# The scores of the first two neighbourhood jobs beside the last projection panels

## The chip, the cores and the metric

The kernel runs on one core of one Trainium2 chip. The metric is the device time of one execution in microseconds; three runs of the kernel before the change took 1579.09, 1581.71 and 1585.59 us, and their median, 1581.71 us, is the time before. The result must agree with a reference in JAX that works in 32-bit floats.

## The reference

Two layers of a diffusion backbone run over 512 latent tokens, on a grid 64 columns wide, and 256 context tokens, with a model width of 1024. Layer 0 projects the modulated tokens once and then attends in two groups of heads: eight latent-attention heads and eight heads of two-dimensional neighbourhood attention. A SwiGLU follows. Layer 1 has sliding-window attention and another SwiGLU. What the change touches is the neighbourhood attention of layer 0. Each latent query reads 16 columns around it, in every one of the grid's eight rows, with a bias by relative place, and all context keys, in one softmax; context queries read context keys alone. Cut to its core:

```python
p_lat = a_lat @ w_in
p_ctx = a_ctx @ w_in
...
s_lat = jnp.einsum('bnqhd,bknmhd->bhnqkm', qr, k_blk).astype(jnp.float32) * scale
s_lat = s_lat + col_bias[:, dr_idx].transpose(0, 2, 3, 1, 4)[None]
s_lat = jnp.where(col_ok[:, :, None, :], s_lat, NEG_INF).reshape(b, h, n_cb, NA_CB, kr * NA_KB)
s_ctx = jnp.einsum('bnqhd,bchd->bhnqc', qr, kc).astype(jnp.float32) * scale
p = jax.nn.softmax(jnp.concatenate([s_ctx, s_lat], axis=-1), axis=-1).astype(v.dtype)
p_lat = p[..., n_ctx:].reshape(b, h, n_cb, NA_CB, kr, NA_KB)
return (jnp.einsum('bhnqc,bchd->bnqhd', p[..., :n_ctx], vc)
        + jnp.einsum('bhnqkm,bknmhd->bnqhd', p_lat, v_blk))
```

## The kernel before

Tokens lie along the free axis, 512 latent and 256 context columns, and features on the 128 partitions. A 32-bit product is made of three matmuls, with both operands split into a rounded part and a rest (L335, L337, L338). The modulated tokens are eight such pairs, sixteen tiles of the pool `b`, which has 24 buffers; they stay until the last projection has read them.

`projections()` is a generator over twelve panels of weights (one of them narrow). A panel is worked on the latent columns (24 matmuls of 512 columns) and on the context columns (24 of 256), and the generator gives up control after every second of eight steps, so a panel has eight steps and all panels have 96. The first four panels make queries and keys of head pairs 0 and 1, the next four feed the latent heads, and the last four are the raw queries and keys of pairs 2 and 3, left in the pool `p` of eight buffers until `split_pair` splits them. Between the steps `bg()` makes the modulation vectors: VectorE multiplies and sums one half of the weights by one vector (L255, L259), GpSimd multiplies in place by the other (L272), ScalarE sums that (L273), and VectorE ends it (L275, L276).

Attention is a row of jobs (`na_jobs`, three for each of four head pairs). Job 0 of a pair does the context queries of both heads, job 1 the latent query blocks 0 and 1, job 2 the blocks 2 and 3. A job is a generator with two halves. Its front makes, for each query block, the scores on TensorE (L745, L746) into one of three banks `pss`, takes them out on VectorE with the bias added and the row minimum found (`take`, L555, into a tile of `p` or `wr`), and makes exponentials on ScalarE with their sum (`exps`, L551). The bias of a head is two tiles `nb`, loaded by DMA into a pool of two buffers; a pair needs four. The context queries of one head share a bank, one half each. After its front a job yields False; its back turns the exponentials on TensorE (L499, into banks `pst` and `psd`, two each), copies them out on VectorE or ScalarE (L490, L491), and multiplies with the values (L545).

`attend()` runs jobs with a lag of one: the front of a job is written beside the back of the one before, by a pattern of f, b and s, where s is a step of side work (the splits of later pairs, the latent norms with the root L988, its reciprocal L989 and the gain L965). Before the change the first front starts when all projections are written.

The order written in the program is a list of priorities. A scheduler goes through it with its own estimate of times and fixes each engine's order and each buffer's tenants; on the chip each engine works its list in order and waits at semaphores.

Of the kernel before, what the change touches and what calls it, by code (L numbers as in the profile page):

```python
# [2 lines left out]

# [1 line left out]

# [63 lines left out]
PATTERN = ("fbsfbsfbbsfs",) * 3  # L69
BG = ((0, 0, 0, 0, 0), (2, 3), (0, 0), (0, 0))  # L70
FIRST = 2000
STEPS = ((2, 3, 4, 4), 5, 3)
HALVES = (slice(0, 256), slice(256, 512))
SWAP8 = [(i // 16) * 16 + (i % 16 + 8) % 16 for i in range(32)]
# [24 lines left out]
def hybrid_kernel(ctx: ExitStack, tc, I, out):  # L99
# [6 lines left out]
    def T(tag, shape, dt=F32):  # L106
        count[0] += 1
        if tag not in SIZES:
            return sb.tile(shape, dt, tag=tag, name=f"{tag}_{count[0]}", bufs=BUFS.get(tag, 1))
        n = int(np.prod(shape[1:]))  # L110
        t = sb.tile([P, SIZES[tag] // (2 if dt == mybir.dt.bfloat16 else 4)], dt, tag=tag, name=f"{tag}_{count[0]}",
                    bufs=BUFS[tag])[: shape[0], :n]
        if len(shape) == 3:
            t = t.rearrange("p (a b) -> p a b", a=shape[1])
        return t

    def B(dt=F32, tag="b"):
        return T(tag, [P, NT], dt)

    def PS(tag):  # L120
        count[0] += 1
        return ps.tile([P, 512], F32, tag=tag, name=f"ps{tag}_{count[0]}", bufs=PBUFS[tag])
# [185 lines left out]
    def bg(n=1):  # L308

        for _ in range(n):  # L310
            next(mods, None)
# [213 lines left out]
    def weighted(o, lanes):  # L525
# [13 lines left out]
        for n in range(max(len(m) for m in moving)):  # L539
            for i, (v, _, all_qs) in [*enumerate(lanes)][::-1]:  # L540
                if n < len(moving[i]):
                    kt, qs, t = moving[i][-1 - n]
                    c = slice((qs[0] - all_qs[0]) * P, (qs[-1] + 1 - all_qs[0]) * P)
                    with shifted(-FIRST):
                        ins = PE.matmul(o[64 * i : 64 * i + 64, c], v(kt), t, start=n == 0, stop=n == len(moving[i]) - 1)  # L545
# [97 lines left out]
    @contextmanager  # L643
    def shifted(by):
        tc.cur_priority += by
        yield
        tc.cur_priority -= by
# [3 lines left out]
    def step(n=1):  # L651

        for _ in range(n):
            while side_work:
                try:
                    with shifted(lower[0]):
                        next(side_work[0])
                    break
                except StopIteration:
                    side_work.popleft()  # L660
# [8 lines left out]
    def attend(jobs, lag=LAG):  # L669

        todo = deque()
        outs[1] = PS("o") if PBUFS["o"] == 1 else None
        for j in jobs:
            n, units = rate[0]
            bg(int(len_jobs[0] * units) - int((len_jobs[0] - 1) * units))
            len_jobs[0] += 1
            pattern = PATTERN[phase[0]]
            sides, back, front = pattern.count("s"), todo.popleft() if len(todo) >= lag else None, True
            i = 0
            for x in pattern:  # L680
                if x == "s":
                    step((i + 1) * n // sides - i * n // sides)
                    i += 1
                elif x == "f":
                    front = front and next(j)
                elif back:
                    back = None if next(back, back) is back else back
            while front:
                front = next(j)
            if back:  # L690
                for _ in back:
                    pass
            todo.append(j)
        for j in todo:
            for _ in j:
                pass
# [45 lines left out]
    def stacked_scores(t1, ks):  # L742
        def scores(o, q, keys):
            x = t1[:, q * P : (q + 1) * P]
            PE.matmul(o, x, ks[0][:, keys], start=True, stop=False)  # L745
            PE.matmul(o, x, ks[1][:, keys], start=False, stop=True)  # L746

        return scores
# [24 lines left out]
    def keys_of(v, side, mixed=None):  # L773

        def get(kt):
            t, i = (v, kt) if kt < 6 else (mixed, kt - 6)
            return t[:, i * P + 64 * side : i * P + 64 * side + 64]

        return get
# [15 lines left out]
    def first_norm(acc, c):  # L795
        n, d = (c.stop - c.start) // P, PM()
        col = T("sm", [P, 6, 2]).rearrange("p a b -> p (a b)")[:, :n]
        ins = [PE.matmul(d[:, i : i + 1], acc[:, i * P : (i + 1) * P], ones[:, :1], start=True, stop=True) for i in range(n)]
        run(ins[0], ins[-1])
        root = S.activation(col, d[:, :n], AF.Sqrt, bias=eps, scale=1.0 / D)  # L800
        V.reciprocal(col, col)
        return root, col
# [74 lines left out]
    _, diag = first_norm(acc, LATS)  # L877
# [8 lines left out]
    for c in range(4):  # L886
# [16 lines left out]
        if c == 3:  # L903
            _, diag = first_norm(acc, CTXS)
# [31 lines left out]
    def beside(gen):  # L936
        side_work.append(gen)
        return gen
# [81 lines left out]
    def split_pair(p):  # L1020

        tag = ("b", "st")[p - 2]
        q, k = raws[2 * p - 4 : 2 * p - 2]
        how = S.copy, G.tensor_copy, V.tensor_copy
        sets.append((new_q(tag), new_k(tag)))
        put_q(sets[p][0], None, how[RQ[p - 2]], (G, V)[RL[p - 2]].tensor_tensor)(q, slice(0, NT))
        yield
        put_k(sets[p][1], KC[1], how[RK[p - 2]])(k, slice(0, NT))
        yield
# [96 lines left out]
    def mix():  # L1126

        t = B()
        for i in range(2):
            VX.append(t[:, 2 * P * i : 2 * P * i + 2 * P])  # L1130
            v = VN[len(VX) - 1]
            for r, c in ((slice(0, 64), slice(2 * P, 4 * P)), (slice(64, 128), slice(0, 2 * P))):
                G.tensor_copy(VX[-1][r], v[r, c])

    def na_jobs():
        for p in range(4):
            if p == 3:
                lower[0] = L3
            for x in ORDER[p]:
                beside(split_pair(int(x)) if x in "23" else {"n": latent_norms, "m": mla_prepare}[x]())  # L1140
            rate[0] = STEPS[0][p], BG[0][p]
            if p % 2 == 0:
                mix()
            po = B()
            sums, mins = T("sm", [P, 6, 2]), T("sm", [P, 6, 2])
            hs = []
            for s in range(2):
                t1, ks = sets[p]
                hs.append(Head(s, stacked_scores(t1[s], ks[s]), keys_of(VN[p], s, VX[p]), None, nb_tiles(2 * p + s), -LOWEST, sums, mins))
            yield from pair_jobs(hs, po, True, finish(po, sums, 6))  # L1150
            while len(sets) < min(p + 2, 4):
                step()
            ON.append(po)

    i = 0
    for _ in projections():
        i += 1
        bg(int(i * DBG) - int(i * DBG - DBG))
    dense[0] = False
    attend(na_jobs())  # L1160
    drain()

    def in_rows(src, dst=None):
# [13 lines left out]
    def mla_jobs():  # L1177
        phase[0], lower[0] = 1, LOWER
        rate[0] = STEPS[1], BG[0][4]
        ready.append(latent_operands(1))  # L1180
# [44 lines left out]
    ahead, soon = {}, []  # L1225
# [378 lines left out]
    lower[0] = LOWER  # L1604
    rate[0] = STEPS[2], 0
    attend(swa_jobs())
# [186 lines left out]
```

## Time and profile before

| what | value |
|---|---|
| median of three runs | 1581.71 us (1579.09 to 1585.59) |
| the profiled execution | 1582.8 us, its span 1581.0 us |
| granted TensorE clock, mean | 0.992 |
| 0 to 46 us, start and first norm: TensorE busy | 31.37 us, clock 0.96 |
| 46 to 176 us, values' end and projections | 128.84 of 130 us, clock 1.00 |
| 176 to 268 us, neighbourhood attention | 85.45 of 92 us, clock 0.94 |
| 268 to 370 us, latent heads | 100.82 of 102 us, clock 1.00 |

The rest, from 370 us on, is the output projection, the first SwiGLU, layer 1 and the second SwiGLU. A span runs from the first to the last instruction of the profiled execution; the device time of the same execution is 1.8 us longer. The clock is the share of full speed that TensorE was granted. A busy TensorE at half the clock counts as busy, so both columns have to be read. Lines are those of the kernel before; in the changed kernel they are two higher at first (L557 is L555, L747 is L745).

### The profile page before, as it was taken

Reading aid. Unit: us, or ns where it says so; the run is one execution under the profiler, and the core shown is the slowest. Engines: PE = TensorE matmul, PEld = TensorE weight load, DVE = VectorE, ACT = ScalarE, POOL = GpSimd, SP = SyncE. Lnnn points to the kernel's source line nnn. Section 1 sums busy time; section 2 is a strip of 40 time slices with the busy share of each in tenths; the row PEclk is TensorE's granted clock in tenths of the full one; section 3 lists DMA queues with packets and bytes.
Section 4 is the critical chain, followed back from the end, with each engine's and each line's share of the span. In section 5 each row is a group of like instructions: output and inputs, shape, how many; then the busy total and the mean of one; then the engine's idle time right before and its main releaser. Section 6 shows DMA issues by size and latency. Waiting matters only on the chain.

```text
span 1581.0 us, 26527 instructions
## 1 busy us (share of the span) xinstructions
PE 1532.9 (97%) x10024; PEld 1376.0 (87%) x10024; DVE 1174.2 (74%) x2345; ACT 795.6 (50%) x1607; POOL 275.9 (17%) x302
## 2 busy tenths in 40 slices
PE   6999999999999999999999999999999999999998
PEld 4787778887998999999989998877789899899998
DVE  3885777685678597786858676889976778678685
ACT  4563677775565243342424334548856545454453
POOL 0144624320011101002021121480012000000001
PEclk9999999999999999999999999999999999999999
DMA  9745242004444545537465585110225123323222
GB/s 313 253 130 175 77 129 73 11 7 160 155 165 144 175 156 181 198 127 273 154 252 176 171 328 191 42 52 2 62 77 170 50 98 128 94 94 127 84 98 87
DMA packets 76464, 214.91 MB, mean 136 GB/s; under 512 B 9872, under 2 KB 16400, under 8 KB 76336
## 3 DMA queue, kind: packets, MB, share of 16 engines
q1 hardware_dynamic: 59216, 144.42, 27.8%
q0 software_dynamic: 15968, 67.24, 12.2%
q8 instruction: 78, 1.28, 0.3%
q10 hardware_dynamic: 1152, 1.57, 0.3%
q14 instruction: 50, 0.41, 0.1%
HBM read 186.97 MB, written 23.07 MB: 133 GB/s over the span
## 4 chain that ended last, share of the span: by engine, by line
PE 38%; DVE 5%; issue 3%; DMA 3%; POOL 1%; ACT 1%; DVEq 0%; POOLq 0%; ACTq 0%
PE pss L1378 3%; PE pss L1376 2%; PE pss L1377 2%; PE pso L545 2%; PE pst L1378 2%; PE pst L1377 2%; PE pst L1376 2%; PE psd L335 2%; DMA rope<-in_mod_w_dram 2%; PE pss L335 2%; PE pss L337 2%; PE pss L338 2%; PE psd L337 2%; PE psd L338 2%; PE pst L337 1%
## 5 line engine op out<-in xcount | busy, mean ns | idle before, releaser
L324 ACT CAST wh<-wr 128x1024 fp32r<-128x1024 f32 (+2 forms) x148 | 115.4, 795 | 204.5 <-DMA wr<-in_w_dn_dram 35.0
L325 DVE TENSOR_TENSOR wl<-wr,wh 128x1024 fp32r<-128x1024 f32 (+2 forms) x145 | 133.8, 930 | 69.2 <-ACT wh L324 68.8
L551 ACT ACTIVATE p<-p,sm 128x512 f32<-128x512 f32 (+3 forms) x144 | 104.9, 730 | 28.8 <-DVE sm L555 27.1
L233 DVE CUSTOM_DVE_ANT_0 p<-rope,cond 128x1024 bf16<-128x1024 f32 x64 | 77.2, 1223 | 42.8 <-DMA rope<-in_mod_w_dram 42.7
L1376 PE MATMUL pss<-b,wh 128*128 128x384 f32 (+1 forms) x346 | 107.7, 312 | 0.6 <-ACT b L361 0.6
L1377 PE MATMUL pss<-b,wh 128*128 128x384 f32 (+1 forms) x346 | 107.9, 312 | 0.1
L1378 PE MATMUL pss<-b,wl 128*128 128x384 f32 (+1 forms) x346 | 106.8, 312 | 1.1 <-DVE wl L1364 1.1
L337 PE MATMUL psd<-b,wh 128*128 128x512 f32 (+3 forms) x262 | 89.7, 342 | 0.0
L335 PE MATMUL psd<-b,wh 128*128 128x512 f32 (+3 forms) x222 | 80.1, 361 | 1.2 <-ACT b L464 0.8
L338 PE MATMUL psd<-b,wl 128*128 128x512 f32 (+3 forms) x222 | 78.7, 355 | 0.0
L545 PE MATMUL pso<-ph,b 128*64 128x256 f32 (+1 forms) x384 | 77.7, 361 | 0.4 <-DVE ph L490 0.4
L545 PE MATMUL pso<-pl,b 128*64 128x256 f32 (+1 forms) x384 | 77.4, 359 | 0.0
L1378 PE MATMUL pst<-b,wl 128*128 128x384 f32 (+1 forms) x226 | 70.8, 313 | 2.4 <-DVE wl L1364 2.4
L1377 PE MATMUL pst<-b,wh 128*128 128x384 f32 (+1 forms) x226 | 70.5, 312 | 0.0
L1376 PE MATMUL pst<-b,wh 128*128 128x384 f32 (+1 forms) x226 | 70.5, 312 | 0.0
L337 PE MATMUL pss<-b,wh 128*128 128x256 f32 (+3 forms) x216 | 69.3, 321 | 0.0
L335 PE MATMUL pss<-st,wh 128*128 128x512 f32 (+2 forms) x198 | 67.1, 339 | 0.4 <-ACT wh L324 0.3
L228 POOL DMA_DIRECT2D rope<-in_mod_w_dram x48 | 25.5, 530 | 241.0 <-DVE mod L233 227.9
L338 PE MATMUL pss<-st,wl 128*128 128x512 f32 (+2 forms) x198 | 67.1, 339 | 0.0
L1378 PEld LDWEIGHTS pss<-b,wl 128*128 128x128 f32 x346 | 65.4, 190 | 1.8 <-DVE wl L1364 1.6
L1376 PEld LDWEIGHTS pss<-b,wh 128*128 128x128 f32 x346 | 65.6, 190 | 1.1 <-ACT b L361 0.9
L1377 PEld LDWEIGHTS pss<-b,wh 128*128 128x128 f32 x346 | 65.6, 190 | 0.8 <-DVE b L362 0.6
(624 smaller groups left out, 5341.2 us busy)
## 6 DMA issues: line engine op xcount, KB each, us to landing
wr<-in_w_gu_dram SPq DMA_DIRECT2D x88, 512.0 KB, 4.0
rope<-in_mod_w_dram POOLq DMA_DIRECT2D x48, 512.0 KB, 3.8
wr<-in_w_dn_dram SPq DMA_DIRECT2D x73, 256.0 KB, 3.1
wr<-in_w_out_dram SPq DMA_DIRECT2D x32, 512.0 KB, 3.5
p<-home POOLq DMA_DIRECT2D x40, 384.0 KB, 5.5
home<-p POOLq DMA_DIRECT2D x40, 384.0 KB, 5.0
wr<-in_w_in_dram SPq DMA_DIRECT2D x21, 512.0 KB, 4.4
nb<-in_nb_dram SPq DMA_DIRECT2D x16, 384.0 KB, 3.2
```

The costliest lines, as they stand in the source:

```text
L228: G.dma_start(w, I["mod_w"][at])
L233: V.tensor_tensor_reduce(out=T("p", [P, D], mybir.dt.bfloat16), in0=w, in1=cond[:, v, :], op0=ALU.mult, op1=ALU.add, scale=1.0, scalar=0.0 ...
L324: behind(S.copy(h, r), *after[:1])
L325: behind((G if eng else V).tensor_tensor(lo, r, f(h), op=ALU.subtract), *after[1:])
L335: ins = PE.matmul(o, wh[:, k], mh[:, c], start=first and k == 0, stop=False)
L337: PE.matmul(o, wh[:, k], ml[:, c], start=False, stop=False)
L338: PE.matmul(o, wl[:, k], mh[:, c], start=False, stop=last and k == n - 1)
L545: ins = PE.matmul(o[64 * i : 64 * i + 64, c], v(kt), t, start=n == 0, stop=n == len(moving[i]) - 1)
L551: S.activation(p[:, c], p[:, c], AF.Exp, bias=nm, scale=-1.0, accum_out=dn)
L1376: PE.matmul(o, wh, xh, start=first and k == 0, stop=False, skip_group_check=not first)
L1377: PE.matmul(o, wh, xl, start=False, stop=False, skip_group_check=not first)
L1378: PE.matmul(o, wl, xh, start=False, stop=k == 3, skip_group_check=not first)
```

## The change

Of the first two jobs, the context queries and the query blocks 0 and 1 of head pair 0, the fronts are written among the projections. `fronts()` takes a job from `na_jobs` and runs it until it yields False. It is stepped after the steps 82, 84, 86, 88, 90, 92 and 94 of the projections, which lie in the last two panels; six steps are the query blocks of the two jobs, the seventh ends the second front. `resumed` gives such a job back to `attend` with a front that ends at once, so that its back runs as before.

```diff
+from itertools import chain
...
+FRONTS = (82, 84, 86, 88, 90, 92, 94)
...
-    i = 0
+    def resumed(j):
+        yield False
+        yield from j
+
+    def fronts():
+        for _ in range(2):
+            early.append(next(jobs))
+            yield from iter(early[-1].__next__, False)
+
+    jobs, early, i = na_jobs(), [], 0
+    ahead = fronts()
     for _ in projections():
         i += 1
         bg(int(i * DBG) - int(i * DBG - DBG))
+        if i in FRONTS:
+            next(ahead, None)
+    for _ in ahead:
+        pass
     dense[0] = False
-    attend(na_jobs())
+    attend(chain((resumed(j) for j in early), jobs))
     drain()
```

The order of the engines differs from the last two panels to the beginning of the latent heads, and is the same after it but for buffer numbers. On TensorE before the change, the last projection (`pst_1773`) ends, and the context scores of the two heads (`pss_1833`, `pss_1843`) and the first near scores (`pss_1871`) follow it:

```order
L335 MATMUL pst_1773<-b_112,wh_1735 128x256
L337 MATMUL pst_1773<-b_113,wh_1735 128x256
L338 MATMUL pst_1773<-b_112,wl_1736 128x256
L745 MATMUL pss_1833<-st_654,st_652 128x256
L746 MATMUL pss_1833<-st_655,st_652 128x256
L745 MATMUL pss_1843<-st_656,st_653 128x256
L746 MATMUL pss_1843<-st_657,st_653 128x256
L745 MATMUL pss_1871<-st_654,st_652 128x256
```

On TensorE after the change, in the panel before the last, whose context columns go to `pss_1725`; `pss_1714` is the first context piece of head 1, and the second piece of head 0 (`pss_1692`) stands eight products behind it:

```order
L340 MATMUL pst_1654<-b_112,wl_1651 128x512
L747 MATMUL pss_1714<-st_656,st_653 128x256
L748 MATMUL pss_1714<-st_657,st_653 128x256
L337 MATMUL pss_1725<-b_98,wh_1650 128x256
...
L339 MATMUL pss_1725<-b_103,wh_1650 128x256
L747 MATMUL pss_1692<-st_654,st_652 128x256
L748 MATMUL pss_1692<-st_655,st_652 128x256
L340 MATMUL pss_1725<-b_102,wl_1651 128x256
```

So products of a projection now stand behind scores in TensorE's queue. On VectorE before the change, the modulation steps run through to the end of the projections without a take (these rows stand at the second half of the panel before the last):

```order
L275 TENSOR_TENSOR mod_294_1377<-part_1632,part_1635 128x1
L276 SCALAR_TENSOR_TENSOR mod_294_1377<-mod_294_1377,modb_89 128x1
L275 TENSOR_TENSOR mod_294_1377<-part_1696,part_1699 128x1
L276 SCALAR_TENSOR_TENSOR mod_294_1377<-mod_294_1377,modb_89 128x1
L255 ISA p_1718,mod_293_1376<-ph_1716,cond_66 128x512
```

On VectorE after the change, at the same place, the takes of the context scores stand between them; an ISA row with a bank `pss` is a take, the row without sources behind it reads the minimum out:

```order
L277 TENSOR_TENSOR mod_294_1377<-part_1632,part_1635 128x1
L278 SCALAR_TENSOR_TENSOR mod_294_1377<-mod_294_1377,modb_89 128x1
L557 ISA p_1693,sm_1683<-pss_1692,zeros_95 128x256
L557 ISA sm_1683 128x1
L277 TENSOR_TENSOR mod_294_1377<-part_1732,part_1735 128x1
L278 SCALAR_TENSOR_TENSOR mod_294_1377<-mod_294_1377,modb_89 128x1
L557 ISA p_1715,sm_1683<-pss_1714,zeros_95 128x256
```

Further on, on VectorE after the change, at the end of the last projection, the near takes of head 1 (`wr_1819`, `p_1841`, with its bias tile `nb_1688`) stand ahead of the key split of pair 2 (L727, L728) and the first copy of turned exponentials (L492):

```order
L557 ISA p_1782,sm_1683<-pss_1775,nb_1684 128x512
...
L557 ISA wr_1819,sm_1683<-pss_1814,nb_1688 128x512
L557 ISA sm_1683 128x1
L557 ISA p_1841,sm_1683<-pss_1834,nb_1688 128x512
L557 ISA sm_1683 128x1
L727 CAST b_1891<-p_1563 64x768
L728 TENSOR_TENSOR b_1892<-p_1563,b_1891 64x768
L727 CAST b_1893<-p_1563 64x768
L492 COPY pl_1912<-pst_1907 128x512
L257 ISA p_1854,mod_293_1376<-ph_1852,cond_66 128x512
```

The split of pair 2 thus moves behind all near takes of query blocks 0 and 1. `nb_1688` takes the buffer of `nb_1684`, which the row of `p_1782` is the last to read.

## The prediction

> **What bounds the kernel now.** I read the page first, then the busy time by stretches of 5 us, then the timelines of TensorE, VectorE and the other engines where the stretches show a hole. The page says which engine sets the time:
>
> ```profile
> PE 1532.9 (97%) x10024; PEld 1376.0 (87%) x10024; DVE 1174.2 (74%) x2345; ACT 795.6 (50%) x1607; POOL 275.9 (17%) x302
> ```
>
> TensorE is busy for 1532.9 of 1581.0 us. The change adds and drops no matmul, so it can only win from the 48.1 us in which TensorE stands idle, and from time at a lowered clock, which the busy time hides. The stretches around the end of the projections (columns: stretch, length, busy us of PE, PEld, DVE, ACT and POOL with their counts, granted clock, DMA share, GB/s):
>
> ```profile
> 160.00:165.00 5.00, 5.00 (x24) 4.13 (x23) 4.96 (x9) 2.40 (x7) 3.67 (x4) 1.00 0.01 5
> ...
> 175.00:180.00 5.00, 3.77 (x25) 2.94 (x24) 4.88 (x11) 4.03 (x9) 4.74 (x5) 1.00 0.50 120
> 180.00:185.00 5.00, 4.63 (x22) 4.63 (x22) 1.71 (x8) 3.23 (x10) 4.76 (x4) 0.54 0.38 98
> 185.00:190.00 5.00, 4.87 (x30) 3.81 (x29) 3.36 (x9) 2.25 (x6) 3.90 (x3) 0.78 0.05 20
> 190.00:195.00 5.00, 3.48 (x24) 2.76 (x24) 2.78 (x11) 4.95 (x10) 3.62 (x2) 1.00 0.71 191
> 195.00:200.00 5.00, 4.94 (x46) 3.93 (x46) 4.97 (x12) 4.37 (x14) 0.00 (x0) 1.00 0.62 166
> ...
> 210.00:215.00 5.00, 2.73 (x16) 1.73 (x14) 4.75 (x12) 3.98 (x9) 1.42 (x1) 0.95 0.66 215
> 215.00:220.00 5.00, 5.00 (x29) 3.62 (x27) 2.85 (x8) 5.00 (x16) 3.20 (x5) 0.71 0.21 56
> ```
>
> From 175 to 200 TensorE loses 1.23 + 0.37 + 0.13 + 1.52 + 0.06 = 3.3 us idle and, at clocks of 0.54 and 0.78, 5 x 0.46 + 5 x 0.22 = 3.4 us of speed: 6.7 us. From 210 to 220 it loses 2.27 us idle and 0.25 + 1.45 = 1.7 us of clock: 4.0 us. The timeline of TensorE names the holes (start, length, instruction, idle before it and what ended it):
>
> ```profile
> 177.82 0.39 PE L745 MATMUL pss<-st,st 128*128 128x256 f32 x1 [0.55 <-DVE sm L555]
> 180.37 0.53 PE L745 MATMUL pss<-st,st 128*128 128x192 f32 x1 [0.85 <-DVE sm L555]
> 193.76 0.39 PE L745 MATMUL pss<-st,st 128*128 128x256 f32 x1 [1.39 <-DVE sm L555]
> 213.90 0.63 PE L499 MATMUL psd<-ident_r,p 128*128 128x128 f32 x4 [1.54 <-DVE b L965]
> ```
>
> The first three are scores (L745) that wait for VectorE to take earlier scores out of PSUM (L555): attention starts with an empty pipeline. The fourth belongs to the latent norms, beside the second pair.
>
> **What moves on TensorE.** The first two jobs hold eight score pieces: two heads with two context pieces of 128x256, then two heads with two near pieces of 128x512. The pace of TensorE comes from these rows:
>
> ```profile
> 164.94 0.28 PE L335 MATMUL pss<-b,wh 128*128 128x256 f32 x1
> 167.81 0.40 PE L335 MATMUL psd<-b,wh 128*128 128x512 f32 x1
> 173.28 0.28 PE L335 MATMUL pst<-b,wh 128*128 128x256 f32 x1
> 176.15 0.28 PE L745 MATMUL pss<-st,st 128*128 128x256 f32 x1
> 189.65 0.33 PE L745 MATMUL pss<-st,st 128*128 128x192 f32 x1
> 190.40 0.38 PE L499 MATMUL pst<-ident_r,wr 128*128 128x128 f32 x2
> ```
>
> Twenty-four products of 256 columns take 167.81 - 164.94 = 2.87 us, 0.12 each; twenty-four of 512 take 5.47 us, 0.228 each. A near piece in three parts takes 190.40 - 189.65 = 0.75 us; one in two parts is four matmuls of 0.12, 0.48 us; a context piece is two, 0.24 us. Together 4 x 0.24 + 2 x 0.48 + 2 x 0.75 = 3.4 us go in front of the projections' end. That is no loss in itself; it comes off the time behind.
>
> A wait comes with it. In the new order, head 0's second context piece stands eight products behind head 1's first, and writes the bank whose first half VectorE must have taken (the 0.55 us row is this same wait). The rows for VectorE, which will set the pace from here (timeline rows, then group rows with count, busy time and mean ns):
>
> ```profile
> 165.15 1.14 DVE L276 SCALAR_TENSOR_TENSOR mod<-mod,modb 128x1 f32<-128x1 f32 x1
> 177.35 0.41 DVE L555 CUSTOM_DVE_ANT_0 p<-pss,zeros 128x256 f32<-128x256 f32 x1
> 190.10 0.69 DVE L555 CUSTOM_DVE_ANT_0 p<-pss,nb 128x512 f32<-128x512 f32 x1
> 193.01 0.69 DVE L555 CUSTOM_DVE_ANT_0 wr<-pss,nb 128x512 f32<-128x512 f32 x1 [2.22 <-DMA nb<-in_nb_dram]
> 197.94 0.95 DVE L982 TENSOR_TENSOR b<-b,b 128x768 f32<-128x768 f32 x1
> 201.58 0.69 DVE L555 CUSTOM_DVE_ANT_0 p<-pss,nb 128x512 f32<-128x512 f32 x1
> 204.94 0.23 DVE L989 RECIPROCAL sm<-sm 128x12 f32<-128x12 f32 x1 [1.80 <-ACT sm L988]
> ...
> 159.39 1.89 DVE L255 CUSTOM_DVE_ANT_0 p<-pl,cond,mod 128x512 bf16<-128x512 f32 x1
> 168.06 0.75 DVE L255 CUSTOM_DVE_ANT_0 p<-pl,cond,mod 128x512 bf16<-128x512 f32 x1
> ...
> L255 DVE CUSTOM_DVE_ANT_0 p<-pl,cond,mod 128x512 bf16<-128x512 f32 x8 | 10.4, 1300 | 0.2
> L255 DVE CUSTOM_DVE_ANT_0 p<-ph,cond 128x512 bf16<-128x512 f32 x8 | 7.8, 971 | 0.0
> L259 DVE SCALAR_TENSOR_TENSOR mod<-mod,modb 128x1 f32<-128x1 f32 x7 | 6.2, 882 | 0.1
> ...
> L490 DVE COPY pl<-pst 128x512 f32<-128x512 f32 x6 | 4.1, 688 | 4.3 <-PE pst L499 4.2
> L726 DVE TENSOR_TENSOR b<-p,b 64x768 fp32r<-64x768 f32 x2 | 2.6, 1290 | 0.0
> L726 DVE TENSOR_TENSOR st<-p,st 64x768 fp32r<-64x768 f32 x2 | 1.9, 949 | 0.0
> L725 DVE CAST b<-p 64x768 fp32r<-64x768 f32 x1 | 0.6, 647 | 0.0
> ```
>
> With the accumulator read a context take costs 0.50 us and a near take 0.76. TensorE reaches the second context piece at 164.94 + 0.48 + 8 x 0.12 = 166.4. On VectorE the first take stands behind the modulation step L276, which ends at 166.29; it is out at 166.8. **New wait: 0.4 us**, with the projection's products queued behind it on TensorE. From 166.8 follow 20 matmuls of 0.12, 5.47 us of products and 0.48 + 0.75 + 0.48 + 0.75 of near pieces: 177.1; then the last 24 products end at 180.0, 3.8 us later than now (176.15). The other pieces find their banks taken long before.
>
> **What moves on VectorE.** I walk its new order. The first near piece is written at 171.0; take, 171.8. Then come a modulation tile (0.97 + 1.30 + 0.16 + 0.88) and the second near take, 175.9. The third near take needs head 1's bias tile, which goes into head 0's buffer (two nb buffers for four tiles); the load costs the 2.22 us of the row above: 178.1. This wait is new here, and idle time of VectorE, not of TensorE. Two takes, 179.6. The key split of a later pair (0.65 + 1.29 + 0.65), 182.2; copy of the first transposes, 182.9; 0.97 + 1.29 + 1.30 of modulation and split, 186.5; three near takes, **188.8**. These leave only head 1's last near take. In the old order the takes up to head 1's last two end at 190.10 + 0.69 = 190.8, and the next waits 2.22 us for its bias tile, which in the new one comes beside other work. So the new order is 2.0 us ahead. Bounds: with the four L255 at 0.75 and the two splits at 0.95, their shortest rows, VectorE needs 2.2 us less and is 4.2 ahead; with two L255 at 1.89 and the L259 at the 1.14 of the row above, 1.5 us more, 0.5 ahead. What slows them is GpSimd's products beside them (a group row):
>
> ```profile
> L272 POOL TENSOR_TENSOR ph<-ph,cond 128x512 f32<-128x512 f32 x7 | 11.4, 1635 | 35.7 <-PE pss L209 30.3 <-DVE mod L255 4.8 <-issue 0.7
> ```
>
> I take the means, since the same products run there again. ScalarE's table load moves with the first exponential into the projections, where no matmul waits for ScalarE.
>
> Up to the second near take of the next pair, six copies (4.1), two near takes (1.5), four context takes (2.0), two splits (1.9) and small ones (0.6) make 10.2 us: 199.0, against 201.58, 2.6 ahead. Then the new order is worse: the bias tile of that pair (2.22 less the 0.95 us add beside it) and the wait for the norms' root (1.80) come one behind the other, 3.1 us, where now they overlap, 1.80 + 0.4 = 2.2. That gives back 0.9: **1.7 us ahead** at the transposes of 213.90. There TensorE has one more near piece behind it (0.75) and VectorE two context takes for one 0.95 us split, so about **2 to 2.5 us** are won in all. Behind this place the order on all engines becomes the same again and TensorE is the bound, so the gain stays; the second dip (4.0 us) hangs on L965 as before, and I leave it.
>
> Of the 6.7 us, then, some 4 go into new waits of TensorE for VectorE between 184 and 190: the hole moves, since VectorE's list is as long as before.
>
> **The clock.** I count no gain from it beyond the walk. It fell after holes of 1.2 and 2.3 us, and elsewhere after 1.47, but not after 1.37:
>
> ```profile
> 975.00:977.50 2.50, 1.03 (x8) 0.80 (x7) 2.50 (x4) 2.35 (x5) 2.23 (x2) 1.00 1.02 383
> 980.00:982.50 2.50, 2.50 (x14) 2.50 (x13) 0.00 (x0) 0.00 (x0) 0.00 (x0) 0.50 0.00 0
> 192.50:195.00 2.50, 1.13 (x7) 0.92 (x8) 1.99 (x7) 2.50 (x6) 2.00 (x2) 1.00 0.74 210
> ```
>
> So another hole of above 1 us may bring it back, at 1.7 us (as at 215) or 3.4 us (as at 180). The Trainium skill (TensorE: Matmul & The Clock Gate, "Part 1: The HAM clock gate") asks for at least one idle window of about 3.4 us before the clock is halved; by it none of these holes would cost clock, and the trace disagrees, with 1.47 us at 975.
>
> **Rivals.** (1) The pipeline starts full and nothing new waits: all 6.7 us, with the dip at 210 gone as well 10.7: 1575.0 to 1571.0. For it: three of the four holes are the empty pipeline. Against: VectorE's list. (2) The clock falls anyway, at the new holes or because transposes (L499) count less as work: 1.7 to 3.4 us go, 1581.2 to 1582.9. By transposes alone it should also fall here, in their own rows:
>
> ```profile
> 220.00:225.00 5.00, 2.27 (x18) 2.04 (x19) 1.00 0.16 14
> ```
>
> and it does not. The same page ("Part 4: PE-mode transpose") says that transposes do not engage the full clock; this row disagrees. (3) Slower: TensorE's queue is in order, and VectorE was busy for 4.96 of the 5 us from 160 to 165. If the first takes run 2 us late there, TensorE waits 2.4 instead of 0.4 us in the midst of products that have no wait now, the clock falls there (3.4 us), and VectorE's walk is 1.5 us longer: 2.0 + 3.4 + 1.5 = 6.9 us against the forecast, 1586.4, or 1584.7 with the shorter dip. It decides from 2.5 us of waits in the projections on. That the change does nothing is excluded by the new order itself.
>
> **How the numbers follow.** Forecast: the profiled run takes 1582.8 us around its span of 1581.0; less 2.2 it is 1580.6, and the median of the runs, 1.1 us below, becomes 1579.5. Chances: forecast (gain 0.5 to 5) 0.55, rival 1 0.18, rival 2 0.17, rival 3 0.10. What a measurement of this kernel can tell from no change is 0.5%, 7.9 us: below 1573.8 lies two thirds of rival 1, 0.13; above 1589.6 the far part of rival 3, 0.05; within, 0.82. The range for 8 in 10 is 1573.8 to 1585: rival 1's weaker half, the VectorE bounds (0.5 to 4.2 ahead), the clock's 1.7 to 3.4.
>
> **What would show it.** Right: near 166 a wait of some 0.4 us before L747 (score) in the projections; projections ending 3.5 to 4 us later; no holes at the start of attention; the table load inside the projections; VectorE waiting some 2 us for nb before the third near take; TensorE waiting for L557 or an exponential about 184 to 190. Wrong: no such holes there (then rival 1), a clock of 0.5 inside 166 to 180 (rival 3), or a shift that is gone by the latent stage.

## The result: slower by 0.25%, and the profile after

| kernel | median | runs | ratio to the kernel before, 95% interval |
|---|---|---|---|
| before | 1583.04 us (1578.4 to 1589.03) | 22 | 1 |
| changed | 1586.95 us (1581.79 to 1592.75) | 22 | 1.0025 [1.0015, 1.0035] |

The change costs 3.9 us where 2.2 of gain were forecast. It lies within 0.5% of the time before, but outside the range given. The busy times on the page of the changed kernel, whose span is 1587.6 us:

```profile
PE 1534.0 (97%) x10024; PEld 1375.9 (87%) x10024; DVE 1180.6 (74%) x2345; ACT 796.5 (50%) x1607; POOL 277.3 (17%) x302
```

TensorE's work is the same. VectorE has the same 2345 instructions as before and is busy 6.4 us longer (1180.6 against 1174.2): the first sign of what happened. The last latent-head scores on TensorE tell where the time went. One row for the kernel before, one for the changed one (line, count, min/median/max in ns, first and last start in us):

```profile
L1119 PE MATMUL pss<-st,st x80: 274/283/398, 258.1 to 367.9; 96*128 96x256 f32 x24, 128*128 128x256 f32 x24, 96*128 96x512 f32 x16, 128*128 128x512 f32 x16
```

```profile
L1121 PE MATMUL pss<-st,st x80: 274/283/402, 265.6 to 372.3; 96*128 96x256 f32 x24, 128*128 128x256 f32 x24, 96*128 96x512 f32 x16, 128*128 128x512 f32 x16
```

The last of them comes 4.4 us later. Of these, 1.2 us were there before the change touches anything: the panel before the last starts at 160.7 instead of 159.5 (its first product on TensorE's timeline). Below, "aligned" means with these 1.2 us taken off. So 3.2 us are lost between that panel and the end of the latent heads. The remaining 2.2 us of the two profiled spans lie behind them, where the order is the same. Seven of the experiments below have the change and leave the modulation's steps at their place; in that part they lie between 1.1 us less and 3.2 us more than before, and five of the seven take 1.7 us or more longer. The profiled execution of the changed kernel took 1589.43 us, 2.5 above the median, so I take this rest as the spread of single executions; no run isolates it.

The stretches of 5 us of the changed kernel in the stage (columns as in the prediction):

```profile
175.00:180.00 5.00, 5.00 (x37) 4.70 (x37) 2.15 (x6) 3.31 (x8) 3.11 (x5) 1.00 0.24 79
180.00:185.00 5.00, 4.83 (x41) 4.50 (x39) 4.90 (x6) 4.92 (x11) 4.26 (x3) 1.00 0.43 118
185.00:190.00 5.00, 1.67 (x12) 0.91 (x12) 4.84 (x9) 1.16 (x2) 2.49 (x2) 1.00 0.44 106
190.00:195.00 5.00, 3.78 (x15) 2.96 (x15) 5.00 (x10) 4.04 (x10) 4.85 (x4) 0.66 0.60 160
195.00:200.00 5.00, 3.64 (x25) 2.93 (x27) 4.93 (x10) 3.01 (x9) 5.00 (x3) 0.74 0.47 130
```

The holes of 176 to 194 are gone; from 185 to 200 there are new and larger ones, 3.33 + 1.22 + 1.36 us, and the clock falls again behind them (0.66 and 0.74). VectorE is busy for 4.84 to 5.00 of each 5 us from 180 on: it is what TensorE waits for, as TensorE's timeline says:

```profile
167.86 0.39 PE L747 MATMUL pss<-st,st 128*128 128x256 f32 x1
186.62 0.33 PE L501 MATMUL pst<-ident_r,wr 128*128 128x128 f32 x1 [1.79 <-DVE pl L492]
190.63 0.80 PE L747 MATMUL pss<-st,st 128*128 128x512 f32 x1 [2.34 <-DVE sm L557]
196.36 0.39 PE L747 MATMUL pss<-st,st 128*128 128x256 f32 x1 [1.42 <-DVE sm L557]
217.13 0.63 PE L501 MATMUL psd<-ident_r,p 128*128 128x128 f32 x4 [0.56 <-DVE b L967]
```

The first row is the score that was to wait in the projections. Behind the product at 167.46 it would have started after 0.12 us, and it starts after 0.40: a wait of 0.28 us.

And this is VectorE's own timeline at the place where the walk of the prediction has the key split of pair 2 (L727, L728) and the three near takes:

```profile
180.12 0.69 DVE L557 CUSTOM_DVE_ANT_0 p<-pss,nb 128x512 f32<-128x512 f32 x1
...
180.73 2.02 DVE L727 CAST b<-p 64x768 fp32r<-64x768 f32 x1
182.85 2.41 DVE L728 TENSOR_TENSOR b<-p,b 64x768 fp32r<-64x768 f32 x1
185.28 0.56 DVE L727 CAST b<-p 64x768 fp32r<-64x768 f32 x1
185.87 0.69 DVE L492 COPY pl<-pst 128x512 f32<-128x512 f32 x1
...
188.31 1.64 DVE L257 CUSTOM_DVE_ANT_0 p<-pl,cond,mod 128x512 bf16<-128x512 f32 x1
...
191.11 0.68 DVE L557 CUSTOM_DVE_ANT_0 p<-pss,nb 128x512 f32<-128x512 f32 x1
...
192.32 1.24 DVE L261 SCALAR_TENSOR_TENSOR mod<-mod,modb 128x1 f32<-128x1 f32 x1
...
194.08 1.62 DVE L728 TENSOR_TENSOR st<-p,st 64x768 fp32r<-64x768 f32 x1
```

The same cast takes 2.02 us at 180.73 and 0.56 at 185.28. GpSimd's timeline shows what stands beside the long ones: the subtractions of the queries' split (L714), the modulation's product (L274), then the norms' squares (L980):

```profile
180.50 3.94 POOL L714 TENSOR_TENSOR b<-p,b 64x768 fp32r<-64x768 f32 x2
187.43 1.98 POOL L274 TENSOR_TENSOR ph<-ph,cond 128x512 f32<-128x512 f32 x1 [2.99 <-issue]
189.48 4.05 POOL L714 TENSOR_TENSOR st<-p,st 64x768 fp32r<-64x768 f32 x2
...
194.85 5.75 POOL L980 TENSOR_TENSOR b<-b 128x768 f32<-128x768 f32 x3
```

Between 184.44 and 187.43 GpSimd is idle, and the cast that lies there has its short duration. Before the change, both casts of the key split ran ahead of the subtractions of the same pair:

```profile
174.19 0.55 DVE L725 CAST b<-p 64x768 fp32r<-64x768 f32 x1 [1.22 <-PE pst L338]
175.34 1.14 DVE L726 TENSOR_TENSOR b<-p,b 64x768 fp32r<-64x768 f32 x1
176.51 0.65 DVE L725 CAST b<-p 64x768 fp32r<-64x768 f32 x1
178.14 1.45 DVE L726 TENSOR_TENSOR b<-p,b 64x768 fp32r<-64x768 f32 x1
```

```profile
178.85 2.41 POOL L712 TENSOR_TENSOR b<-p,b 64x768 fp32r<-64x768 f32 x1
```

### The profile page after: what moved, and what is told of

The parts are those of the page before. It is cut to its first block, busy times and chain, and to the rows that moved or that the text cites. A ratio compares the mean times of both kernels' runs of the same rounds, so it can differ in the third digit from the quotient of the medians.

```text
span 1587.6 us, 26516 instructions
## 1 busy us (share of the span) xinstructions
PE 1534.0 (97%) x10024; PEld 1375.9 (87%) x10024; DVE 1180.6 (74%) x2345; ACT 796.5 (50%) x1607; POOL 277.3 (17%) x302
## 5 line engine op out<-in xcount | busy, mean ns | idle before, releaser
L327 DVE TENSOR_TENSOR wl<-wr,wh 128x1024 fp32r<-128x1024 f32 (+2 forms) x145 | 133.8, 930 | 68.7 <-ACT wh L326 68.3
```

Source lines behind the costliest of these rows:

```text
L327: behind((G if eng else V).tensor_tensor(lo, r, f(h), op=ALU.subtract), *after[1:])
```

## The experiments

Two reasons for the loss were put against each other. **G**: GpSimd's work holds VectorE's instructions up, and the change puts the key split exactly beside it. **L**: VectorE's list is simply too long in the last panels, whatever stands beside it. A third, **V**, blamed the place of the key split in the order. Each run was timed beside the kernel before on the same chip. Lines of kernels with an edit can be one or two off.

**Only the first job early.**

```diff
-FRONTS = (82, 84, 86, 88, 90, 92, 94)
+FRONTS = (82, 84, 86)
...
-        for _ in range(2):
+        for _ in range(1):
```

> Only the first job's front (the four context pieces) is made beside the projections; the second job's front goes back behind them. Theory V (VectorE is the late one: the near takes of the second job push the key split of pair 2 and the first copies behind the projections, where GpSimd's products of the same split slow them): the split goes back to where it stood, the first two holes of TensorE stay away, and the kernel is 1 to 4 us faster than before (ratio 0.9975 to 0.9995). Rival C (scores among the projections cost by themselves, by waits in TensorE's queue and the clock): half of the cost stays, 1 to 3 us slower than before.

Measured: 1584.29 against 1582.28 us, 1.0013 [1.0000, 1.0026]: about half of the loss (2.0 us of 3.9) stays, where V expected 1 to 4 us of gain. The key cast takes its old 0.60 us in the mean (1.2 us for two, as before), the key subtraction 1.34 (1.29 before). So the key split doesn't explain this half. It doesn't arise at the start of attention either: over the 50 us of the table further below TensorE loses 6.1 us here, against 6.7 before. The trace shows a hole of TensorE later on, for a copy on VectorE that stands behind two casts (VectorE's row, then TensorE's):

```profile
236.76 5.01 DVE L1107 CAST st<-b 32x768 fp32r<-32x768 f32 x2
242.27 0.58 PE L757 MATMUL psd<-wh,b 128*128 128x256 f32 x1 [2.62 <-DVE b L492]
```

GpSimd works beside them from 236.12 to 241.35. Before the change the same two casts take 2.98 us in the same place, and TensorE has no such hole; two others, at 225.43 and 227.33, take 0.55 us each. So what is left of the loss here can be the same kind of hold-up at a later place; no run tests that.

**The key split later in the order.**

```diff
-ORDER = ("2", "n3", "m", "")
+ORDER = ("", "2n3", "m", "")
```

> The changed kernel with the split of pair 2 moved from the side work of head pair 0 to that of pair 1. Theory V: VectorE has 5 to 6 us less to do between 180 and 190 us, the waits of TensorE of 1.79 and 2.34 us there shrink to under 1 us in sum, and the time is 2 to 6 us below the changed kernel's (from 2 us above before to 2 us below). Rival N (the bias tiles in two buffers set the pace): the holes stay, 3 to 5 us slower than before.

Measured: 1587.75 us, 1.0035 [1.0022, 1.0047], no better than the change as made, where V expected 2 to 6 us less. The casts take 1.51 us each there; TensorE's hole only moves, to 3.59 us at 191. A later place doesn't help. As GpSimd's subtractions and squares stand beside the split there too, this run doesn't part V from G.

**No modulation in the last two panels.**

```diff
-        bg(int(i * DBG) - int(i * DBG - DBG))
+        bg(int(i * DBG) - int(i * DBG - DBG) if i < 80 else 0)
```

> The changed kernel with no background step of the modulation in the last two panels; the vectors left over are made later, on demand. Theory V: L257, L261 and L274 go out of 172 to 195 us, VectorE has some 4 us less to do between 180 and 195, the holes there shrink by 2 to 4 us; the time goes to 1 us above or 2 below before, if the later place costs nothing. Rival N: the holes stay, and the time is 3 to 5 us above before.

Measured: 1592.02 us, 1.0062 [1.0046, 1.0077]. This total says nothing of the stage by itself, for the vectors left out are then made when they are first needed: from the first output added to the residual (L1218) to the first product of the SwiGLU (L1376) it takes 100.9 us, before the change 95.1. The trace does say something of the stage: from the start of the panel before the last to the last latent-head scores it takes 205.9 us, against 208.4 before and 211.6 as made, although its key split takes 11.1 us, longer than as made. A shorter list of VectorE helps there too. A later pair of runs puts the vectors in a better place.

**Head 1's first bias tile in a buffer of its own.**

```diff
-        ts = [T("nb", [P, NT]) for i in range(2)]
+        ts = [T("wr" if h == 1 and i == 0 else "nb", [P, NT]) for i in range(2)]
```

> The changed kernel with one of head 1's two bias tiles in a buffer of the weights' pool (three, free here), so that it loads early. Theory V: the third near take no longer waits for its tile, but VectorE idled there anyway; within 1.5 us of the changed kernel, 2.5 to 5.5 us above before. Rival N (bias tiles): 2 to 4 us below the changed kernel, 0 to 2 us above before.

Measured: 1585.09 us, 1.0015 [1.0002, 1.0028]. The loss is 2.8 us in place of 3.9, with intervals that overlap. The third near take and the key split begin earlier there, and the split of pair 2 takes 4.8 us in place of 6.0. So the bias load may have a part in the loss; the intervals don't tell whether, or how much.

**The split's subtractions and the squares off GpSimd**, in the changed kernel and in the one before. VectorE takes four subtractions, ScalarE the squares:

```diff
-RK, RQ, RL, SQ = (2, 0), (0, 0), (0, 0), 1
+RK, RQ, RL, SQ = (2, 0), (0, 0), (1, 1), 0
```

> The changed kernel with GpSimd's work beside the start of attention given to others: the four subtractions of the query splits go to VectorE, the three squares of the latent norms to ScalarE. Theory G (VectorE is held up by GpSimd beside it; its operations there took 2.02, 2.41, 1.64, 1.62 us instead of 0.6 to 0.95): VectorE gets 3.8 us more of its own and loses some 6 us of hold-up, the holes between 185 and 200 us shrink, the time is 1.5 to 3.5 us below the changed kernel's, 0.5 to 2.5 us above before. Rival L (VectorE's own list is too long there, whoever works beside it): 3.8 us more on it make the time 2 to 4 us longer than the changed kernel's, 6 to 8 us above before.

> The same edit on the kernel before. Theory G: there TensorE waits less for VectorE (VectorE stood idle for 3.8 and 2.2 us in the same stretch), so the edit wins little, within 2 us of before. Rival L: 1 to 3 us slower than before.

Measured: 1587.85 us (1.0027 [1.0011, 1.0043]) for the changed kernel, 1589.26 (1.0042 [1.0024, 1.0059]) for its twin. The casts are at 0.55 us again, as G says. But VectorE has 3.8 us more to do (four rows of 0.95), and the total stays, between what G and L expected. The twin is 7.0 us slower than the kernel before, more than either expected. Against its twin the change is 1.4 us faster here, against 3.9 slower as made; the two intervals overlap, so this alone doesn't decide.

**The modulation of the last two panels beside the latent heads**, in both kernels:

```diff
-BG = ((0, 0, 0, 0, 0), (2, 3), (0, 0), (0, 0))
+BG = ((0, 0, 0, 0, 0.38), (2, 3), (0, 0), (0, 0))
...
-        bg(int(i * DBG) - int(i * DBG - DBG))
+        bg(int(i * DBG) - int(i * DBG - DBG) if i < 80 else 0)
```

> The changed kernel with the six background steps of the last two panels made beside the latent heads instead, where VectorE is busy for 72 of 102 us. Theory G (and L): the projections' end and the start of attention win some 5.7 us against the changed kernel, as in the run without these steps; beside the latent heads 0 to 2 us are lost; 1 to 4 us faster than before. Rival D (the modulation has to be paid wherever it stands): 2 to 5 us slower than before.

> The same edit on the kernel before. Theory G: the modulation steps stood in VectorE's way only where takes stand beside them, which is hardly so before the change: the edit wins at most 2 us, and the changed kernel with it is then the faster of the two, by 1 to 3 us. Rival: the edit wins as much here, 4 to 6 us, and the change is a loss with it too.

Measured: 1583.73 us (1.0015 [0.9998, 1.0032]) and 1583.64 (1.0011 [0.9995, 1.0028]). With the modulation elsewhere the change costs nothing against its twin. It doesn't win either, where 1 to 3 us against the twin were expected, and the group rows of the changed kernel with this edit say why:

```profile
L728 DVE TENSOR_TENSOR b<-p,b 64x768 fp32r<-64x768 f32 x2 | 4.1, 2064 | 0.1
L727 DVE CAST b<-p 64x768 fp32r<-64x768 f32 x2 | 4.1, 2042 | 0.0
L728 DVE TENSOR_TENSOR st<-p,st 64x768 fp32r<-64x768 f32 x2 | 2.9, 1438 | 0.0
```

The key split of both pairs takes 11.1 us here, and 1.9 + 1.9 + 1.2 = 5.0 in the twin's group rows: the whole hold-up now falls on it.

**GpSimd cleared at no cost to VectorE**, in both kernels. The squares go to ScalarE, the queries' subtraction becomes a copy on ScalarE, the modulation's product is left out:

```diff
-RK, RQ, RL, SQ = (2, 0), (0, 0), (0, 0), 1
+RK, RQ, RL, SQ = (2, 0), (0, 0), (0, 0), 0
...
-                G.tensor_tensor(w, w, cond[:, 1, c], op=ALU.mult)
...
-                    (lo or G.tensor_tensor)(t[x, c], src[r], f(t[r, c]), op=ALU.subtract)
+                    S.copy(t[x, c], src[r])
```

> The changed kernel with GpSimd cleared at no cost to VectorE: the queries' split writes a second copy on ScalarE in place of GpSimd's subtraction, the squares of the latent norms are ScalarE's, and the modulation's products on GpSimd are left out (three parts of the computation are changed, so that its time alone counts). Theory G (GpSimd's products hold up VectorE's instructions, which is why my walk by mean durations came out late): the key cast is back at about 0.6 us and the key subtraction at 0.95 to 1.3 us, and this kernel is 0 to 2.5 us faster than its twin, the kernel before with the same three edits. Theory L (VectorE's list is too long in the last panels, whatever stands beside it): it stays 3 to 4 us slower than its twin.

> The kernel before with the same three edits: the twin of the run with GpSimd cleared. Both theories: within 4 us of the kernel before (VectorE freed of hold-up, ScalarE with some 5 us more work beside the stage). Only the difference to the twin tells: G 0 to +2.5 us slower than the twin, L 3 to 4 us faster than it.

Measured: the changed kernel with these edits 1576.26 us (0.9964 [0.9952, 0.9976]), its twin 1581.51 (0.9989 [0.9978, 1.0000]). With nothing beside VectorE the change **wins 5.2 us**, and the intervals are apart; with GpSimd's work there it loses 3.9. L alone falls, for by it the change would have stayed 3 to 4 us slower, though the runs before show that a longer list costs too. G stands, with a reservation: the edits also give ScalarE more to do and change the scheduled order. The twin has a hole of TensorE of 2.09 us for an exponential on ScalarE (at 180.08), so not all of the 5.2 us need come from VectorE. VectorE's timeline of the cleared changed kernel, the same instructions as above:

```profile
178.82 0.55 DVE L726 CAST b<-p 64x768 fp32r<-64x768 f32 x1
179.47 0.95 DVE L727 TENSOR_TENSOR b<-p,b 64x768 fp32r<-64x768 f32 x1
180.45 0.56 DVE L726 CAST b<-p 64x768 fp32r<-64x768 f32 x1
...
183.48 0.75 DVE L257 CUSTOM_DVE_ANT_0 p<-pl,cond,mod 128x512 bf16<-128x512 f32 x1
...
185.98 0.68 DVE L556 CUSTOM_DVE_ANT_0 p<-pss,nb 128x512 f32<-128x512 f32 x1
...
186.59 0.16 DVE L261 SCALAR_TENSOR_TENSOR mod<-mod,modb 128x1 f32<-128x1 f32 x1
```

From the first cast to the start of the third near take are 7.16 us; as made, 180.73 to 191.11, 10.38. TensorE's largest hole in this stretch is then 0.78 us, and the clock stays (the first fence is the cleared changed kernel, the second its twin):

```profile
185.00:190.00 5.00, 3.81 (x21) 2.51 (x23) 5.00 (x15) 4.96 (x12) 0.00 (x0) 1.00 0.56 137
```

```profile
175.00:180.00 5.00, 2.28 (x16) 1.82 (x15) 4.84 (x16) 4.93 (x11) 1.09 (x2) 0.99 0.59 139
180.00:185.00 5.00, 4.92 (x24) 4.92 (x24) 0.80 (x3) 3.02 (x11) 0.00 (x0) 0.50 0.36 98
```

Summed over the ten stretches of 5 us from the start of the panel before the last, TensorE's idle time and the speed lost at a lowered clock (stretch times one less the clock) are, in us:

| kernel | idle | clock | together | key split, both pairs |
|---|---|---|---|---|
| before | 3.3 | 3.4 | 6.7 | 5.7 |
| changed | 6.2 | 3.4 | 9.6 | 9.2 |
| cleared, before | 3.9 | 3.4 | 7.3 | 5.4 |
| cleared, changed | 2.4 | 0.0 | 2.4 | 4.9 |
| changed, no products | 7.5 | 6.8 | 14.3 | 10.4 |
| changed, no subtractions | 3.2 | 1.7 | 4.9 | 4.9 |

The two cleared kernels differ by 4.9 in the sum and 5.2 in the median. The last two rows come from the runs that follow, and for them the first 50 us don't tell the median. Over 24 such stretches, 120 us, the sums are 7.2 (cleared, changed), 11.1 (cleared, before), 11.7 (before), 14.2 (only the first job early), 16.0 (changed), 18.2 (no products) and 18.5 (no subtractions). That is the order of the medians against the kernel before.

**Which of GpSimd's works, and a complete version.** The last three runs take the products alone away, the subtractions and squares alone, and try a version that leaves nothing out: the modulation beside the latent heads, with the split's subtractions on VectorE and the squares on ScalarE.

```diff
 (products alone)
-                G.tensor_tensor(w, w, cond[:, 1, c], op=ALU.mult)
 (subtractions and squares alone)
-RK, RQ, RL, SQ = (2, 0), (0, 0), (0, 0), 1
+RK, RQ, RL, SQ = (2, 0), (0, 0), (0, 0), 0
-                    (lo or G.tensor_tensor)(t[x, c], src[r], f(t[r, c]), op=ALU.subtract)
+                    S.copy(t[x, c], src[r])
 (complete version)
-RK, RQ, RL, SQ = (2, 0), (0, 0), (0, 0), 1
+RK, RQ, RL, SQ = (2, 0), (0, 0), (1, 1), 0
-BG = ((0, 0, 0, 0, 0), (2, 3), (0, 0), (0, 0))
+BG = ((0, 0, 0, 0, 0.38), (2, 3), (0, 0), (0, 0))
-        bg(int(i * DBG) - int(i * DBG - DBG))
+        bg(int(i * DBG) - int(i * DBG - DBG) if i < 80 else 0)
```

> The changed kernel with only the modulation's products on GpSimd left out (so its modulation vectors of the second column are wrong; its time alone counts). If these products are what holds VectorE up, most of the 10.7 us between the changed kernel and its cleared form come back here: 5 to 9 us faster than the changed kernel, 1 to 5 faster than the kernel before. If it is the queries' subtractions and the squares, 0 to 4 us faster than the changed kernel.

> The changed kernel with the queries' subtractions replaced by copies on ScalarE and the squares moved to ScalarE, the modulation's products kept on GpSimd (the low parts of the first pairs' queries are wrong; its time alone counts). The complement of the run without products: 5 to 9 us faster than the changed kernel if the subtractions and squares hold VectorE up, 0 to 4 if the products do. The run that gave VectorE the subtractions instead won nothing; if this one wins 4 us or more, the 3.8 us of list were what ate it there.

> The changed kernel with the six modulation steps moved out of the last panels to the latent heads, the queries' subtractions given to VectorE and the squares to ScalarE: nothing left out, and GpSimd is nearly empty while the first jobs run. Hold-up (theory G): VectorE pays 3.8 us for four subtractions of 0.95 but loses none of its waits on GpSimd, and the stage keeps some of the 5 us that the cleared twin won: 1 to 3 us faster than the kernel before. If it is only the sum of VectorE's work that counts: as the run with the modulation beside the latent heads, plus up to 3.8 us, 1 to 6 us slower than the kernel before.

Measured: without products 1586.90 us, 1.0030 [1.0016, 1.0045]; without subtractions and squares 1586.97, 1.0038 [1.0021, 1.0054]; the complete version 1588.28, 1.0049 [1.0031, 1.0067]. Neither half wins anything in the median, where both together win some 10 us (1.0025 against 0.9964 of the time before): the two don't add up, and my expectations that one of them would win 5 to 9 were wrong. The complete version is some 7 us slower than the kernel before, where 1 to 3 us of gain or 1 to 6 of loss were expected. The traces say why the halves don't win. Without products, the key split of pair 2 stands beside the subtractions and squares for its whole length (timeline of VectorE, then of TensorE):

```profile
177.60 1.97 DVE L726 CAST b<-p 64x768 fp32r<-64x768 f32 x1
179.68 2.40 DVE L727 TENSOR_TENSOR b<-p,b 64x768 fp32r<-64x768 f32 x1
182.11 2.05 DVE L726 CAST b<-p 64x768 fp32r<-64x768 f32 x1
```

```profile
184.94 0.33 PE L500 MATMUL pst<-ident_r,wr 128*128 128x128 f32 x1 [3.25 <-DVE pl L491]
191.06 0.80 PE L746 MATMUL pss<-st,st 128*128 128x512 f32 x1 [3.64 <-DVE sm L556]
```

Without subtractions the first 50 us do come out well (4.9 us lost against 9.6), so the subtractions and squares count most at this place. The gain goes 25 us later, in one hole (TensorE, then VectorE):

```profile
214.45 1.09 PE L501 MATMUL psd<-ident_r,p 128*128 128x128 f32 x4 [5.85 <-DVE b L967]
```

```profile
210.52 2.46 DVE L364 TENSOR_TENSOR b<-b,b 128x768 fp32r<-128x768 f32 x1 [2.48 <-ACT b L363]
212.91 2.18 DVE L967 SCALAR_TENSOR_TENSOR b<-b,mla_gain,psd 128x512 f32<-128x512 f32 x4
```

In this kernel the scheduler puts the first split behind the norms (L364) in front of the gains (L967) for which TensorE waits, as it did before the change; in the cleared kernel and in the change as made it stands behind them. The split is held up as well: it takes 2.46 us, with GpSimd's split of weights (L327) beside it from 209.83 to 212.17, where it took 0.95 before the change. What an edit does to that order is part of every such difference. Of the complete version this much is seen: its key split is short (0.95 us per subtraction), it loses 3.1 us idle and 5.1 of clock in the first 50 us, with a hole of 2.90 us at 189.08 for a copy behind VectorE's longer list. It gives VectorE's list what it takes from GpSimd, as the earlier pair did. So no complete version that was run beats the kernel before, and whether one exists stays open: the 1576.26 us belong to a kernel that leaves work out.

## Why the prediction was wrong

**The step that failed** is the pricing of VectorE's list, "I take the means, since the same products run there again". The same products run, but not at the same moments: the change moves the key split until it stands beside the queries' subtractions. Against the walk, with 1.2 us added for the later start:

| step of the walk | forecast, aligned | measured |
|---|---|---|
| first near take out | 173.0 | 173.0 |
| second near take out | 177.1 | 176.3 |
| two takes behind it | 180.8 | 180.7 |
| key split of pair 2 (0.65 + 1.29 + 0.65) | 183.4 | 185.8 (2.02 + 2.41 + 0.56) |
| three near takes out | 190.0 | 191.8 |
| transposes behind the gains | 213.4 | 217.1 |

Up to the key split the walk holds within 0.8 us, and then loses 2.4 us on three instructions. The forecast for the transposes is the 213.90 of before less the 1.7 us ahead, plus 1.2. That the three takes come only 1.8 late is owed to 0.69 + 0.96 + 1.64 us where 0.97 + 1.29 + 1.30 were counted, and to takes that start 0.61 behind one another. They are then 0.2 us ahead of the old order, not 2.0. From there to the transposes the forecast gave back 0.3 us (2.0 ahead to 1.7), and 2.2 were lost (0.2 ahead to 2.0 behind): L261 and two L728 take 1.24 + 1.62 + 1.64 us beside GpSimd, 2.4 more than 0.16 and twice 0.95. The groups from 160 to 230 us sum it up for the change as made:

```profile
L257 DVE CUSTOM_DVE_ANT_0 p<-pl,cond,mod 128x512 bf16<-128x512 f32 x4 | 6.1, 1534 | 0.1
L261 DVE SCALAR_TENSOR_TENSOR mod<-mod,modb 128x1 f32<-128x1 f32 x4 | 3.7, 936 | 0.1
L728 DVE TENSOR_TENSOR b<-p,b 64x768 fp32r<-64x768 f32 x2 | 3.4, 1681 | 0.1
L728 DVE TENSOR_TENSOR st<-p,st 64x768 fp32r<-64x768 f32 x2 | 3.3, 1630 | 0.0
L727 DVE CAST b<-p 64x768 fp32r<-64x768 f32 x2 | 2.6, 1286 | 0.0
```

These five groups took 5.2, 2.8, 2.6, 1.9 and 1.2 us before: 5.4 us more. The miss of the forecast is 6.1 us (2.2 forecast, -3.9 measured).

**The bounds of that step were one-sided in effect.** For "0.5 ahead" I let two modulation steps be slow and left the split at its mean. The slow side should have taken every instruction that can be held up at the longest row of its kind. The split's own longest rows before the change, 0.65 and 1.45, would not have been enough; another cast of that trace (L1105) shows the size, with 0.55 us at 225.43 and 1.89 at 238.80. The cleared kernel reaches the other bound: aligned to the kernel before (its panel starts at 159.2), its three takes are out at 187.0, 3.8 us ahead of 190.8, with 4.2 as the bound.

**What was right.** The wait in the projections is 0.28 us, forecast at 0.4. The projections end at 181.1, 3.7 us later when aligned, against 3.8. The holes at the start of attention are gone, and TensorE waits instead for a copy and a take from 185 on, as listed. VectorE waits before the third near take, 1.32 us where some 2 were listed:

```profile
179.50 0.69 DVE L557 CUSTOM_DVE_ANT_0 wr<-pss,nb 128x512 f32<-128x512 f32 x1 [1.32 <-PE pst L340]
```

The row names a product of the last projection, which this take doesn't read. The scores that it reads had ended at 178.37, and its bias tile had been issued at 176.36; these loads land 2.9 to 3.3 us after their issue. With the tile in a buffer of its own, the take follows its scores at once, 3.2 us earlier counted from the start of the panel. So this is the wait for the bias tile that was forecast, with the take at 179.3 when aligned. The table load runs inside the projections, hidden (ScalarE's timeline):

```profile
168.23 1.28 ACT L553 ACT_TABLE_LOAD   x1
```

The 3.2 us lost by the end of the latent heads stay: TensorE is the bound behind them.

**The later waits.** The later bias wait, forecast at 2.2, was 2.39, and the wait for the norms' root, forecast at 1.80, was 1.23: these terms held within 0.6 us.

**The rivals.** Rival 3 gave 1584.7 to 1586.4 us, closest to the result, but by another mechanism: waits of over 2.5 us in the projections, where 0.28 was seen. Rival 2 is half true: the clock falls again, behind the new holes, and the stage loses 3.4 us of it as before. But the clock isn't the difference between the two kernels. Rival 1, a start without new waits, is what the cleared kernel shows: 2.4 us lost in the first 50 us in place of 6.7.

Two readings under the clock and rival 2 are weaker than they look. The holes of 1.2 and 2.3 us are sums over a stretch, with 0.85 and 1.54 us as the longest single waits. At 975 the hole of 1.47 us is followed by 32 products of one column (L387, 5.46 us), and the clock falls while they run, so that the hole alone needn't be the reason. What remains is the fall to 0.54 after 180, behind waits of at most 0.85 us. And the stretch of 18 transposes at full clock has 19 other products in it, so it doesn't tell what transposes do alone.

The Trainium skill (SBUF — State Buffer, "Who interferes with whom") says that VectorE and GpSimd share a pair of ports as an exclusive lock that is held for a whole instruction, that VectorE's casts and its operations with two inputs in SBUF can be blocked by it, and those with at most one input there, outside its two-port modes, cannot. The traces agree: the cast goes from 0.55 to 2.02 us and the subtraction from 0.95 to 2.41 beside GpSimd, while a near take, which reads one tile from PSUM and one from SBUF, takes 0.68 or 0.69 us in every row shown here. With that rule the two ends of each duration could have been put to moments, by laying GpSimd's list beside VectorE's.

## What to carry to other kernels

A duration read from a trace belongs to what stood beside it: if a change moves work on one of two engines that hold each other up, its list must be priced twice, at the shortest and at the longest rows, and the other engine's list walked along with it. A move that fills TensorE's queue early buys nothing while the engine that feeds it is full; first see whether its instructions run at their short durations. And two causes that hide each other have to be removed together in an experiment, since each alone may show nothing.

## What was not expected of the hardware

How large the hold-up is: the same cast of 64x768 took 0.55 us with GpSimd idle and up to 2.05 beside it, the subtraction 0.95 and up to 2.41, and the addition on a single column (L261) 0.16 and 1.24. And taking GpSimd's products away made the stage worse (14.3 us lost against 9.6), with the subtractions and then the squares beside all of the key split of pair 2 (its two casts take 1.97 and 2.05 us).
